# Weight tiles of 4352 bytes in place of 4224: where matmul operands begin in SBUF

## The chip, the cores and the metric

The kernel runs on one core of a Trainium2 chip. The metric is the time of one execution on the device in microseconds (us), where lower is better. The engines are named as the profile names them: PE is TensorE (matmuls), PEld its loading of weights, DVE is VectorE, ACT is ScalarE, POOL is GpSimd, SP is SyncE, which here only issues DMA transfers. SBUF is the on-chip memory of 128 partitions. An address below is a byte offset within a partition, and "remainder" is such an address modulo 256.

## The reference

The reference is one layer of an encoder block over 256 tokens of 2048 channels, in float32. Cut to its matrix products:

```python
hn = rmsnorm(h, mix_norm_pre)
proj = hn @ w_in                         # 2048 -> z 1024, xbc 1536, dt 32, u 1024
y_ssd = ssd_mixer(z, xbc, dt_raw, ...)   # bidirectional Mamba-2 scan, two chunks of 128 tokens
y_pool = pool_mixer(u, pool_w, pool_scale)
h = h + rmsnorm(concat(y_ssd, y_pool) @ w_out, mix_norm_post)
up = rmsnorm(h, ffn_norm_pre) @ w_ffn_up             # 2048 -> 2 x 5632
ff = (gelu(conv3(gate)) * val) @ w_ffn_down          # 5632 -> 2048
h = h + rmsnorm(ff, ffn_norm_post)
gate = sigmoid(rmsnorm(h, ple_norm_pre) @ w_ple_gate)    # 2048 -> 2048
h = h + rmsnorm(gate * (p @ w_ple), ple_norm_post)
```

## The kernel before

**Products in three parts.** TensorE multiplies operands of the type `float32r`, to which a float32 value is rounded. To keep the accuracy of float32, every weight matrix and every activation is split into a high part (the value rounded to `float32r`) and a low part (what is left), and a product is the sum of high x high, high x low and low x high. `split` (line 140) does it for weights: a raw weight tile arrives by DMA, ACT writes the high part with a copy (line 149), and DVE writes the low part with a subtraction (line 150).

**Where the parts lie.** `split` takes one tile for each part, from two groups of five buffers each in the pool `weights`: tag `whi` for high parts and `wlo` for low ones, 1056 float32 values (4224 bytes) a tile. 4224 is 16 x 256 + 128, so neighbouring buffers begin at remainders 128 apart. The built program before has them here:

| buffers | address of the first | remainders of the five |
|---|---|---|
| `raw` (3 of 8192 bytes) | 30560 | 96, 96, 96 |
| `whi` (5 of 4224 bytes) | 55136 | 96, 224, 96, 224, 96 |
| `wlo` (5 of 4224 bytes) | 76256 | 224, 96, 224, 96, 224 |
| pages (13 of 8192 bytes), `mid` (3 of 4096), `hs` (2 of 4096) | 97376 and up | 96 |
| `pth`, `ptl`, the gain tile | 18240 and up | 64 |
| `ident` | 16544 | 160 |

The two groups turn together, so the high and the low part of one weight tile always lie at opposite remainders: of 410 tiles that are split into these buffers, 246 have the high part at 96 and the low part at 224, and 164 the other way round. All other matmul operands that are split (the activation panels, the spare tiles below, `hs`) lie in pages or in `hs`, at remainder 96. Slices of operands begin at multiples of 512 bytes, with one exception: in the first projection (`dtu`) a tile's three slices begin 1408 bytes apart.

**Stages in order.** Two forms of product carry nearly all the time.

- Token-major (`token_major`, line 242): the activations are stationary (128 x 128), the weights are the moving operand, 512 columns at a time. It serves z, the output projection (`wo`, accumulators `woa`), the down-projection (`dn`, accumulators `dna`), ple and the gate (`gt`). A weight block is 256 rows by 1024 columns. Its products stand by tile, by half of the tokens `t`, by part `q`, and then by the two column halves, so that two products in a row use the same stationary operand. In the last block (and for the gate's second half in the last four) the order is by accumulator instead, and the stationary operand changes at every product. The down-projection does 13 of its 44 blocks with seven products in place of eight (`seven_products`, line 203; accumulators `dns` too): 21 matmuls instead of 24.
- Feature-major: the weights are stationary, the activations move. `feature_major` (line 270) does the `xbc` projection with 256 columns. `feature_pairs` (line 287) does the up-projection of the feed-forward (accumulators `ga` for the gate half, `va` for the value half; weight tiles named `ug` and `uv`): the panel `wox` holds the high and low parts of a slice side by side, so a high part of the weights is multiplied with 512 columns (high and low) and the low part with 256. A weight tile gives eight such pairs.

```python
mm(acc[f], wh[:, s], get.both(k), k == 0, False)
mm(acc[f][:, L:], wl[:, s], get(k)[0], False, k == NK - 1)
```

**Spare tiles.** In the second half of the gate, four weight tiles (two blocks) take their high and low parts from pages that are free by then (line 887): in the profile `gth` and `gtl`. They and the ordinary tiles of that stage (`gt_0h`, `gt_0l`, `gt_1h`, `gt_1l`) are multiplied with the same panel `dnx` in one unbroken series at the end.

**Order of the work.** The program is traced once, and a scheduler fixes each engine's order from dependences and buffers. Weights come by DMA from SP's queue into `raw`, three transfers ahead. Two more names in the change are `half_up`, a column of 0.5 that POOL uses at the very end (line 864), and `dynamic_dma_scratch_size`, the bytes at the start of SBUF that are set aside for descriptors of DMAs written by software (16384 when nothing is said).

Of the kernel before, what the change touches and what calls it, by code (L numbers as in the profile page):

```python
# [11 lines left out]
F32 = mybir.dt.float32  # L12
F32R = mybir.dt.float32r
# [3 lines left out]
P = 128  # L17
# [34 lines left out]
def build(nc, a, out):  # L52
# [5 lines left out]
    with tile.TileContext(nc) as tc, \  # L58
# [8 lines left out]
        def ins(r):  # L67
            return getattr(r, "ins", r)

        def page(name, dtype=F32):  # L70
            return gp.tile([P, 2048], dtype, tag="pg", bufs=13, name=name)
# [43 lines left out]
        def load(dst, src, ahead=False):  # L115

            with tc.issue_after(last["dma"]) if last and not ahead else nullcontext():
                return ins(nc.sync.dma_start(dst, src))
# [21 lines left out]
        def split(name, src, nel, cuts=()):  # L140

            if name in spare:
                hi, lo = spare.pop(name)
            else:
                hi = wp.tile([P, 1056], F32R, tag="whi", bufs=5, name=f"{name}h")
                lo = wp.tile([P, 1056], F32R, tag="wlo", bufs=5, name=f"{name}l")
            for c0, c1 in zip((0, *cuts), (*cuts, nel)):
                s = slice(c0, c1)
                last["act"] = ins(nc.scalar.copy(hi[:, s], src[:, s]))
                last["dve"] = ins(nc.vector.tensor_sub(lo[:, s], src[:, s], hi[:, s].bitcast(F32)))  # L150
            return hi, lo
# [51 lines left out]
        def seven_products(name, r, a_, acc, alt, start, stop):  # L203

            v = r.rearrange("p (b c) -> p b c", b=4)
            b11 = split(f"{name}a", r[:, :512], 512)
            b2 = split(f"{name}b", r[:, 1024:], 1024)

            nc.vector.tensor_sub(v[:, 0:2], v[:, 1::2], v[:, 0:2])
            nc.vector.tensor_sub(v[:, 3], v[:, 3], v[:, 0])
            nc.vector.tensor_sub(v[:, 2], v[:, 2], v[:, 3])
            t13 = split(f"{name}c", r[:, :1024], 1024)
            t42 = split(f"{name}d", r[:, 1024:], 1024)
            for x, (wh, wl), c, o, own in (
                    ("a11", b11, 0, alt[0], True), ("a12", b2, 0, acc[0][0], False), ("s4", b2, 512, acc[0][1], False),
                    ("s1", t13, 0, alt[1], True), ("s3", t13, 512, alt[2], True), ("a22", t42, 0, acc[1][0], False),
                    ("s2", t42, 512, alt[3], True)):
                xh, xl = a_[x]  # L220
                for q, (xx, ww) in enumerate(((xh, wh), (xh, wl), (xl, wh))):
                    mm(o, xx, ww[:, c:c + 512], own and start and q == 0, own and stop and q == 2)
# [111 lines left out]
        def row_rstd(name, src):  # L334

            r = []
            for t in range(2):
                q = tiny(f"{name}q{t}", 1)
                junk = page(f"{name}j{t}")
                nc.scalar.activation(junk, src[t], AF.Square, accum_out=q)  # L340
                r.append(rms(f"{name}{t}", [q], 1.0 / D))
            return r
# [86 lines left out]
        with tc.issue_after(half[0]), tc.issue_after(half[1]):  # L429
            xs_ = [page(f"x{t}") for t in range(2)]  # L430
            for t in range(2):
                load(xs_[t], x[t * P:(t + 1) * P, :])
            rx = row_rstd("rx", xs_)
            seg_w = page("seg_w", F32R)[:64, :].rearrange("p (a q s) -> p a q s", a=4, q=4)
            seg_x = page("seg_x", F32R)[:64, :].rearrange("p (a i l) -> p a i l", a=4, i=4)
            for a_ in range(4):
                nc.scalar.activation(seg_w[:32, a_], four[:32].unsqueeze(2).to_broadcast([32, 4, P]), AF.Copy,
                                     scale=-1.0)
                nc.scalar.copy(seg_x[32:, a_], among[32:].unsqueeze(2).to_broadcast([32, 4, P]))
            aneg = ep.tile([P, 32], F32, name="aneg")  # L440
            nc.scalar.activation(aneg, alog, AF.Exp)
            nc.gpsimd.tensor_scalar(aneg, aneg, -1.0, None, op0=ALU.mult)


            pt = page("pt")[:, :512].rearrange("p (k t) -> p k t", k=2)
            load(pt, a["p_t"])
            pth = cp.tile([P, 2, L], F32R, name="pth")
            ptl = cp.tile([P, 2, L], F32R, name="ptl")
            nc.scalar.copy(pth, pt)
            nc.vector.tensor_sub(ptl, pt, pth.bitcast(F32))  # L450
# [308 lines left out]
        h = [page(f"h{t}") for t in range(2)]  # L759
# [91 lines left out]
        vg = [page(f"vg{t}") for t in range(2)]  # L851
        sq = [[], []]

        half_up = cp.tile([P, 1], F32, name="half_up")
        nc.gpsimd.memset(half_up, 0.5)

        def rest_of(o):

# [88 lines left out]


# [14 lines left out]
```

## Time and profile before

| what | value |
|---|---|
| median of 3 runs | 1144.94 us (1144.43 to 1145.71) |
| profiled execution, first to last instruction (span) | 1144.3 us |
| mean granted clock of TensorE | 0.994 |
| busy PE / DVE / ACT / POOL | 1127.1 / 818.4 / 614.2 / 79.3 us |
| matmuls | 6049 records |
| up-projection of the feed-forward | 320 to 798 us of the span |
| down-projection | 798 to 1029 us |

The profile page and the views of the trace come from one execution, whose own time is its span; the page gives no other. In a row of the view in order of time stand the start (us from the span's start), the duration (us), the engine, the line, the operation, output <- inputs (buffer numbers left out), the shape and a count. Durations of matmuls overlap, so the distance from one start to the next says how fast PE goes on. Line 86 is the helper `mm`, through which all matmuls go; the tiles tell them apart.

### The profile page before, as it was taken

What the parts mean: (1) busy time and instruction counts of PE and PEld (TensorE: products, weight loads), DVE (VectorE), ACT (ScalarE), POOL (GpSimd) and SP (SyncE); (2) the same over time, 40 slices, a digit from 0 to 9 for tenths busy, and PEclk for the clock granted to TensorE, in tenths of its full rate; (3) what the DMA queues carried; (4) which work ended last, traced back from release to release, by engine and by line L of the source; (5) the groups of instructions that cost most, each with busy time, mean ns of one, the idle gap of its engine ahead of it and who ended that gap; (6) DMA issues with size and microseconds to landing.
All of it is one profiled execution on the core that took longest, in us unless ns stands there. A gap on an engine that the chain in (4) does not pass through costs nothing.

```text
span 1144.3 us, 15384 instructions
## 1 busy us (share of the span) xinstructions
PE 1127.1 (98%) x6049; PEld 970.4 (85%) x6049; DVE 818.4 (72%) x1067; ACT 614.2 (54%) x837; POOL 79.3 (7%) x91
## 2 busy tenths in 40 slices
PE   9999999999999999999999999999999999999996
PEld 9998888888888888888888888888888888887885
DVE  6659985754876666665766756668888888898573
ACT  6746543553674554554544545545655655667462
POOL 0201105200110000000000000000000000002001
PEclk9999999999999999999999999999999999999998
DMA  9942366556456555555555555556556746654752
GB/s 357 374 149 74 100 245 221 171 170 198 148 185 214 190 185 184 184 187 194 193 190 193 184 184 184 184 195 220 170 188 220 221 147 221 209 195 147 226 179 74
DMA packets 129592, 219.04 MB, mean 191 GB/s; under 512 B 3696, under 2 KB 96752, under 8 KB 128624
## 3 DMA queue, kind: packets, MB, share of 16 engines
q1 hardware_dynamic: 129232, 217.70, 57.2%
q8 instruction: 47, 0.77, 0.3%
q10 hardware_dynamic: 288, 0.36, 0.1%
q14 instruction: 25, 0.20, 0.0%
HBM read 215.95 MB, written 2.10 MB: 191 GB/s over the span
## 4 chain that ended last, share of the span: by engine, by line
PE 95%; DVE 2%; ACT 1%; POOL 1%; issue 1%; DMA 0%; POOLq 0%; DVEq 0%; ACTq 0%
PE va L86 21%; PE ga L86 21%; PE dna L86 17%; PE woa L86 8%; PE gt L86 7%; PE xbc L86 5%; PE dtu L86 4%; PE z L86 4%; PE dns L86 3%; PE pw L86 1%; PE ple L86 1%; PE yd L86 0%; DVE h L740 0%; PE seg L86 0%; DMA dtur<-w_in 0%
## 5 line engine op out<-in xcount | busy, mean ns | idle before, releaser
L86 PE MATMUL ga<-wox,ug_0h 128*128 128x512 f32 x352 | 125.5, 395 | 0.0
L86 PE MATMUL ga<-wox,ug_1h 128*128 128x512 f32 x352 | 125.1, 394 | 0.0
L86 PE MATMUL va<-wox,uv_0h 128*128 128x512 f32 x352 | 124.8, 393 | 0.0
L86 PE MATMUL va<-wox,uv_1h 128*128 128x512 f32 x352 | 124.8, 393 | 0.0
L86 PE MATMUL ga<-wox,ug_0l 128*128 128x256 f32 x352 | 99.1, 282 | 0.0
L86 PE MATMUL ga<-wox,ug_1l 128*128 128x256 f32 x352 | 99.1, 282 | 0.0
L86 PE MATMUL va<-wox,uv_0l 128*128 128x256 f32 x352 | 99.1, 281 | 0.0
L86 PE MATMUL va<-wox,uv_1l 128*128 128x256 f32 x352 | 99.1, 281 | 0.0
L86 PEld LDWEIGHTS va<-wox,uv_0h 128*128 128x128 f32 x352 | 66.1, 188 | 15.0
L86 PEld LDWEIGHTS va<-wox,uv_1h 128*128 128x128 f32 x352 | 66.1, 188 | 15.0
L86 PEld LDWEIGHTS ga<-wox,ug_1h 128*128 128x128 f32 x352 | 66.1, 188 | 14.9
L86 PEld LDWEIGHTS ga<-wox,ug_0h 128*128 128x128 f32 x352 | 66.1, 188 | 14.8
L86 PE MATMUL dna<-dn_0h,hs 128*128 128x512 f32 x248 | 75.8, 393 | 0.0
L86 PE MATMUL dna<-dn_1h,hs 128*128 128x512 f32 x248 | 75.6, 393 | 0.0
L86 PEld LDWEIGHTS ga<-wox,ug_0l 128*128 128x128 f32 x352 | 66.2, 188 | 0.1
L86 PEld LDWEIGHTS ga<-wox,ug_1l 128*128 128x128 f32 x352 | 66.2, 188 | 0.0
L86 PEld LDWEIGHTS va<-wox,uv_0l 128*128 128x128 f32 x352 | 66.2, 188 | 0.0
L86 PEld LDWEIGHTS va<-wox,uv_1l 128*128 128x128 f32 x352 | 66.2, 188 | 0.0
L781 POOL TENSOR_TENSOR fc<-fc,rfb 128x1024 f32<-128x1024 f32 x11 | 26.5, 2408 | 440.1 <-ACT fc L780 440.1
L86 PEld LDWEIGHTS dna<-dn_1h,hs 128*128 128x128 f32 x248 | 46.5, 188 | 10.8
L86 PEld LDWEIGHTS dna<-dn_0h,hs 128*128 128x128 f32 x248 | 46.5, 188 | 10.7
L86 PE MATMUL dna<-dn_0l,hs 128*128 128x512 f32 x124 | 40.2, 393 | 0.0
(1078 smaller groups left out, 2824.0 us busy)
## 6 DMA issues: line engine op xcount, KB each, us to landing
dn0r<-w_ffn_down SPq DMA_DIRECT2D x22, 1024.0 KB, 5.5
dn1r<-w_ffn_down SPq DMA_DIRECT2D x22, 1024.0 KB, 5.5
zr<-w_in SPq DMA_DIRECT2D x8, 1024.0 KB, 5.1
wo0r<-w_out SPq DMA_DIRECT2D x8, 1024.0 KB, 5.4
wo1r<-w_out SPq DMA_DIRECT2D x8, 1024.0 KB, 5.4
gt0r<-w_ple_gate SPq DMA_DIRECT2D x8, 1024.0 KB, 5.6
gt1r<-w_ple_gate SPq DMA_DIRECT2D x8, 1024.0 KB, 5.5
dtur<-w_in SPq DMA_DIRECT2D x14, 528.0 KB, 8.9
```

The source lines that it names most:

```text
L86: nc.tensor.matmul(o, lhsT, rhs, start=start, stop=stop, skip_group_check=True)
L781: nc.gpsimd.tensor_tensor(cv.rearrange("p (f t) -> p f t", f=4), cv.rearrange("p (f t) -> p f t", f=4), rfb.unsqueeze(1).to_broadcast([P, ...
```

## The change

The tiles of `whi` and `wlo` get 1088 values in place of 1056. A tile then takes 4352 bytes, 17 x 256, and all ten buffers begin at the same remainder. What is written to a tile and read from it stays: at most 1056 values. The ten tiles take 1280 bytes more; to make room, the software descriptors' area is halved to 8192 bytes, which moves every tile down. `half_up` (32 bytes with its padding) is taken from the pool of constants before `pth`, `ptl` and the gain tile and not after them, which leaves the remainder of everything behind the constants as it was and moves these three.

```diff
-                hi = wp.tile([P, 1056], F32R, tag="whi", bufs=5, name=f"{name}h")
-                lo = wp.tile([P, 1056], F32R, tag="wlo", bufs=5, name=f"{name}l")
+                hi = wp.tile([P, 1088], F32R, tag="whi", bufs=5, name=f"{name}h")
+                lo = wp.tile([P, 1088], F32R, tag="wlo", bufs=5, name=f"{name}l")
...
             load(pt, a["p_t"])
+            half_up = cp.tile([P, 1], F32, name="half_up")
+            nc.gpsimd.memset(half_up, 0.5)
             pth = cp.tile([P, 2, L], F32R, name="pth")
...
-        half_up = cp.tile([P, 1], F32, name="half_up")
-        nc.gpsimd.memset(half_up, 0.5)
...
-    nc = bacc.Bacc("TRN2", target_bir_lowering=False, num_devices=1)
+    nc = bacc.Bacc("TRN2", target_bir_lowering=False, num_devices=1, dynamic_dma_scratch_size=8192)
```

The addresses in the built program after:

| buffers | address of the first | remainders |
|---|---|---|
| `raw` | 22368 | 96 |
| `whi` | 46944 | 96, 96, 96, 96, 96 |
| `wlo` | 68704 | 96, 96, 96, 96, 96 |
| pages, `mid`, `hs` | 90464 and up | 96 |
| `pth`, `ptl`, the gain tile | 10080 and up | 96 |
| `ident` | 8352 | 160 |

No instruction changes its place on any engine, and none changes what it waits for. The one that the diff seems to move is the memset of `half_up`; on POOL it stood among the first instructions already. Before:

```order
L91 MEMSET mhalf 128x4
masks.py:197 MEMSET ident 128x128
L855 MEMSET half_up 128x1
masks.py:199 ISA
masks.py:199 AFFINE_SELECT ident<-ident 128x128
```

And after:

```order
L91 MEMSET mhalf 128x4
masks.py:197 MEMSET ident 128x128
L448 MEMSET half_up 128x1
masks.py:199 ISA
masks.py:199 AFFINE_SELECT ident<-ident 128x128
```

Only the line number differs.

## The prediction

> **What bounds the kernel.** I read the page first (busy shares, granted clock, chain), then PE's waits, then PE's rows in order of time, because a PE that is always busy can only become faster by shorter instructions.
>
> ```profile
> span 1144.3 us, 15384 instructions
> PE 1127.1 (98%) x6049; PEld 970.4 (85%) x6049; DVE 818.4 (72%) x1067; ACT 614.2 (54%) x837; POOL 79.3 (7%) x91
> PEclk9999999999999999999999999999999999999998
> q1 hardware_dynamic: 129232, 217.70, 57.2%
> q10 hardware_dynamic: 288, 0.36, 0.1%
> PE 95%; DVE 2%; ACT 1%; POOL 1%; issue 1%; DMA 0%; POOLq 0%; DVEq 0%; ACTq 0%
> ...
> L86 PE MATMUL ga<-wox,ug_0h 128*128 128x512 f32 x352 | 125.5, 395 | 0.0
> ...
> L86 PE MATMUL ga<-wox,ug_0l 128*128 128x256 f32 x352 | 99.1, 282 | 0.0
> ```
>
> PE is busy for 98% of the span at nearly full granted clock, and 95% of the chain is PE. Its longest waits are small and stand at changes of stage:
>
> ```profile
> PE gt L86 <- DVE gt_1l L150: 2.3, 1, 2.3
> PE xbc L86 <- DVE xb_0l L150: 2.0, 1, 2.0
> ```
>
> So the time is the number of matmuls times the distance between their starts, which I call the pitch. The duration in the page (395 ns) is no pitch, since matmuls overlap. The pitch has to be read from start times, over many instructions, since a row gives 0.01 us.
>
> The change touches only where operands begin. "Remainder" below is the byte address modulo 256. Before, the ten weight buffers begin at 96 and 224 in turn, and a tile's high and low parts always lie at opposite ones. Pages, panels and `hs` all begin at 96. If the remainder matters, the trace of before must show it already. It does, in two places.
>
> First, the up-projection (lines 770 to 789). Each weight tile feeds eight pairs of a 512-column product with its high part and a 256-column product with its low part, weights stationary. The rows are the first product of consecutive tiles; the built program has their high parts at 96, 224, 96, 224, 96:
>
> ```profile
> 561.09 0.39 PE L86 MATMUL va<-wox,uv_1h 128*128 128x512 f32 x1
> 563.87 0.39 PE L86 MATMUL va<-wox,uv_0h 128*128 128x512 f32 x1
> 566.68 0.39 PE L86 MATMUL va<-wox,uv_1h 128*128 128x512 f32 x1
> 569.46 0.39 PE L86 MATMUL va<-wox,uv_0h 128*128 128x512 f32 x1
> 572.28 0.39 PE L86 MATMUL va<-wox,uv_1h 128*128 128x512 f32 x1
> ```
>
> The tiles take 2.78, 2.81, 2.78 and 2.82 us: 347 ns a pair with the high part at 96, 352 with it at 224. Averaged over all whole tiles the same reading gives 347.0 (102 tiles) and 352.0 (68). Address alone makes 5 ns.
>
> Second, the last stage holds the only weights that lie at 96 in both parts: the spare tiles `gth` and `gtl`, which are pages. Their products alternate with those of ordinary tiles, on the same panel. First comes a run of 12 from spare tiles, then 12 from ordinary ones (the last row starts the next run):
>
> ```profile
> 1118.72 0.39 PE L86 MATMUL gt<-gth,dnxh 128*128 128x512 f32 x1
> ...
> 1121.44 0.39 PE L86 MATMUL gt<-gt_0h,dnxh 128*128 128x512 f32 x1
> ...
> 1124.20 0.39 PE L86 MATMUL gt<-gth,dnxh 128*128 128x512 f32 x1
> ...
> 1129.79 0.28 PE L86 MATMUL gt<-gtl,dnxh 128*128 128x256 f32 x1
> ...
> 1131.11 0.28 PE L86 MATMUL gt<-gt_0h,dnxh 128*128 128x256 f32 x1
> ```
>
> All operands alike: 2.72 us over 12, 226.7 ns each. Mixed: 2.76 over 12, 230.0 each. The 256-column products of the spare tiles, all alike, take 1.32 us over 11, 120.0 each. These are my prices of "after".
>
> **The change part by part.** *Token-major stages, 512 columns.* The weights are the moving operand here. The mean pitch before comes from the first and last row of an unbroken stretch:
>
> ```profile
> 149.76 0.63 PE L86 MATMUL z<-z_0h,hnh 128*128 128x512 f32 x2
> 171.48 0.63 PE L86 MATMUL z<-z_1h,hnl 128*128 128x512 f32 x2
> ...
> 229.94 0.48 PE L86 MATMUL woa<-wo_0h,cath 128*128 128x512 f32 x1
> 296.35 0.40 PE L86 MATMUL woa<-wo_1h,catl 128*128 128x512 f32 x1
> ...
> 798.41 0.63 PE L86 MATMUL dna<-dn_0h,hs 128*128 128x512 f32 x2
> 1028.90 0.40 PE L86 MATMUL dna<-dn_0l,hs 128*128 128x512 f32 x1
> ```
>
> z: 94 pitches in 21.72 us (the second row merges two products and begins with the first), 231.1. wo: 287 in 66.41, 231.4. dn: 998 in 230.49, 231.0 (what lies between two rows is counted in the order of the program). The code issues 192, 384 and 1017 of them, and the gate stage 300 beside the spare ones; gate is priced as z.
>
> - dn: 1017 x (231.0 - 226.7) = 4.4 us.
> - wo: 384 x 4.7 = 1.8 us.
> - z and gate: 492 x 4.4 = 2.2 us.
>
> *Up-projection.* It issues 1408 pairs (four groups of 352 as quoted). By the built program 848 have the high part at 96 and 560 at 224, so the mean is (848 x 347.0 + 560 x 352.0) / 1408 = 349.0. No row shows a pair with all three operands alike. I bound it by the nearest rows, within one tile at 224 (starts of its first three 512-column products, and the next tile's):
>
> ```profile
> 563.87 0.39 PE L86 MATMUL va<-wox,uv_0h 128*128 128x512 f32 x1
> 564.21 0.40 PE L86 MATMUL va<-wox,uv_0h 128*128 128x512 f32 x1
> 564.57 0.40 PE L86 MATMUL va<-wox,uv_0h 128*128 128x512 f32 x1
> ```
>
> Its first pair takes about 0.34 us and its second about 0.36; the recorded starts in nanoseconds have 346 and 358, and later ones 352, 347, 351, 353, 358, 352. So the pitch there wanders, while a tile at 96 holds 346 to 348 throughout. Ends: 345 (lowest seen) and 358 (highest). I take 226.7 + 120.0 = 346.7, the sum of the two alike runs, because both of those hold one steady value, and so does the 347.0 tile; the wandering appears only where the high part is off. Gain: 1408 x (349.0 - 346.7) = 3.2 us, with ends of +5.6 and -12.7.
>
> *256-column products with alike operands.* Here the price goes up:
>
> ```profile
> 52.78 0.36 PE L86 MATMUL xbc<-hnh,xb_0h 128*128 128x256 f32 x1
> 64.15 0.28 PE L86 MATMUL xbc<-hnh,xb_1l 128*128 128x256 f32 x1
> 0.00:52.00 52.00, 49.87 (x302) 49.25 (x303) 31.54 (x42) 38.91 (x56) 7.01 (x16) 1.00 0.98 364
> ```
>
> 95 pitches in 11.37 us, 119.7 against 120.0: 576 x 0.3 is 0.2 us lost, and about 0.1 more for the gate stage's shorter products.
>
> *First projection (`dtu`).* Its slices begin 1408 bytes apart, which is 5 x 256 + 128, so the middle one stays off the others. The last row above, a stretch with its DMA share (0.98) and GB/s at the end, says that the DMA engines set this stage. Nothing taken.
>
> *Scratch, `half_up`, tile sizes.* The two DMA kinds quoted above that move data are hardware ones; nothing is issued that the halved scratch serves, so it costs 0. The memset keeps its place on POOL, and its new address moves `pth`, `ptl` and the gain tile from remainder 64 to 96; the 48 products of ple are too few to price. Tiles are larger by unused bytes: no instruction reads more. No instruction and no wait moves.
>
> *Cover.* A faster PE needs weights sooner. The tightest place in dn is this one:
>
> ```profile
> 891.68 1.22 DVE L150 TENSOR_TENSOR dn_1l<-dn0r,dn_1h 128x1024 fp32r<-128x1024 f32 x1
> 894.97 0.39 PE L86 MATMUL dna<-dn_1l,hs 128*128 128x512 f32 x1
> 798.00:1029.00 231.00, 231.00 (x1003) 187.76 (x1002) 200.86 (x240) 137.39 (x172) 0.91 (x2) 1.00 0.60 196
> ```
>
> The low part is ready at 892.90 and used at 894.97, 2.07 us later. VectorE is busy 200.9 of 231 us in dn, and would be so for 200.9 of 226.6. By the same two kinds of rows its lead swings between 2.1 and 8.4 us with a period of three weight blocks (24 + 24 + 21 products), over which PE gains 69 x 4.3 = 0.3 us. So the cover holds; if it did not, VectorE would be late next.
>
> **Sum.** 4.4 + 1.8 + 2.2 + 3.2 - 0.3 = 11.3 us off the span of 1144.3. The median of the runs, 1144.94, lies 0.6 above that span; I take the same off it: 1133.6.
>
> A rule speaks against all this. The Trainium skill, "SBUF — State Buffer", section "Who interferes with whom", gives TensorE two independent read ports, one for the moving operand and one for the weight load, and says that PE never waits on anyone; its section "Operand start alignment" calls the element-size rule one of legality and says that its runs timed nothing. By that rule the time would stay at 1144.9. The trace disagrees: 347 against 352 ns for the same products.
>
> **The rivals.**
> - *Up-projection gains nothing.* The alike pair settles near today's mean of 349.0. For: its 512- and 256-column products alternate, as in no alike run. Time 1144.9 - 8.1 = 1136.8.
> - *Up-projection takes the wandering pitch.* In the tiles at 224 the low part lies at 96, as it will in all tiles, and its load runs beside the 512-column stream at 96. All pairs at 352.0: 1408 x 3.0 = 4.2 lost, 1141.0. Against: the high part's load then also lies at 96, as in the steady tiles.
> - *Slower: the up-projection locks onto the bad phase.* Each pair takes 358, the worst of the wandering ones: 1408 x 9.0 = 12.7 lost against 8.1 gained, 1149.5. The whole change loses from a pair of 349.0 + 8.1 / 1.408 = 354.8 on, and by over 0.2% from 356.4.
> - *The two-column order does not hold 226.7.* The spare run changes its stationary operand at every product; most of dn, wo, z and gate uses one for two columns. Only the up-projection gains: 1142.
> - *The remainder does nothing* and the 5 ns come from which buffer it is: 1144.9. Against: three different buffers at 96 read the same 347.
>
> **How the numbers follow.** The forecast gets 0.55: of the four regular patterns read above that change weights at every product or pair, three hold a steady pitch (512 alike, 256 alike, high part at 96) and one wanders. No gain in the up-projection gets 0.15, the wandering pitch 0.13, no hold in two-column order 0.05, no effect 0.07, slower 0.05. A difference of 0.2% (2.3 us) is about what runs of this kernel tell from none (they lie within 1.3 us). Faster by more: 0.55 + 0.15 + 0.13 + 0.05 = 0.88; same 0.07; slower 0.05. The first three cases hold 0.83, so the range runs from the 345 end of the up-projection (2.4 us below the forecast, rounded in to 1131.5) to 1141.5.
>
> **What would show it.** In the profile of after: dn from its first to its last product some 4.4 us shorter, at 226.7 a product; the stretch of wo likewise; tiles of the up-projection all equal, near 2.77 us (2.82 means the wandering pitch, 2.86 the bad phase); xbc at 120; PE's waits unchanged. I am wrong if the ordinary tiles of the gate stage still differ from the spare ones, or if a wait of PE for VectorE appears in dn.

## The result: 1142.4 us, and two groups of times

The changed kernel has a median of 1142.39 us over 18 executions (1133.63 to 1144.54); the kernel before, run beside it, has 1144.88 us (1144.26 to 1147.81). The ratio of the two sets is 0.9967 with an interval of 0.9953 to 0.9981 (the medians alone give 0.9978): faster by 0.2 to 0.3%, and not by the 1% that was forecast. The forecast of 1133.6 and its upper end of 1141.5 both lie below the median.

The 18 times do not spread evenly. Three are 1133.63, 1134.11 and 1135.15; the other fifteen lie from 1141.54 to 1144.54; nothing lies between. The forecast is the time of the smaller group. The profiled execution belongs to it: its time is 1133.63 us at a span of 1131.8. First its page: spans, busy shares, granted clock by slice, and the chain.

```profile
span 1131.8 us, 15384 instructions
PE 1115.5 (99%) x6049; PEld 964.9 (85%) x6049; DVE 817.4 (72%) x1067; ACT 613.8 (54%) x837; POOL 79.6 (7%) x91
PEclk9999999999999999999999999999999999999998
PE 95%; DVE 2%; ACT 1%; POOL 1%; issue 1%; POOLq 0%; DVEq 0%; ACTq 0%
```

As many instructions as before, as much work on DVE, ACT and POOL, and 11.6 us less on PE. PE's rows in order of time show the ends of the three stretches read in the prediction (z, wo, dn), of xbc, and of two runs of 12 at the end of the gate stage:

```profile
52.13 0.36 PE L86 MATMUL xbc<-hnh,xb_0h 128*128 128x256 f32 x1
63.61 0.28 PE L86 MATMUL xbc<-hnh,xb_1l 128*128 128x256 f32 x1
...
147.87 0.40 PE L86 MATMUL z<-z_0h,hnh 128*128 128x512 f32 x1
169.21 0.62 PE L86 MATMUL z<-z_1h,hnl 128*128 128x512 f32 x2
...
227.00 0.47 PE L86 MATMUL woa<-wo_0h,cath 128*128 128x512 f32 x1
292.18 0.39 PE L86 MATMUL woa<-wo_1h,catl 128*128 128x512 f32 x1
...
791.05 0.63 PE L86 MATMUL dna<-dn_0h,hs 128*128 128x512 f32 x2
1017.31 0.39 PE L86 MATMUL dna<-dn_0l,hs 128*128 128x512 f32 x1
...
1106.27 0.39 PE L86 MATMUL gt<-gth,dnxh 128*128 128x512 f32 x1
...
1108.99 0.39 PE L86 MATMUL gt<-gt_0h,dnxh 128*128 128x512 f32 x1
...
1111.71 0.39 PE L86 MATMUL gt<-gth,dnxh 128*128 128x512 f32 x1
```

With the same counts of pitches as before: z 21.34 us / 94 = 227.0 ns (before 231.1), wo 65.18 / 287 = 227.1 (231.4), dn 226.26 / 998 = 226.7 (231.0), and xbc 11.48 / 95 = 120.8 (119.7). At the end of the gate stage 12 products of spare tiles and 12 of ordinary tiles now take 2.72 us alike, 226.7 ns each; the ordinary ones took 230.0 before.

The up-projection is best read from the chain, which puts 128 products of `ga` or of `va` (64 pairs) into a row. Of the kernel before and then of the changed one, start, length and what:

```profile
351.86 22.33 PE ga L86 x128
```

```profile
325.29 22.19 PE va L86 x128
347.48 22.19 PE ga L86 x128
```

22.33 us over 64 pairs are 348.9 ns; 22.19 are 346.7. So in this execution the two large terms of the forecast are there. What the forecast misses is in the executions that the profile doesn't show.

### The profile page after: what moved, and what is told of

Read it like the earlier page. It is cut to its first block, busy times and chain, and to the rows that moved or that the text cites. A ratio compares the mean times of both kernels' runs of the same rounds, so it can differ in the third digit from the quotient of the medians.

```text
span 1131.8 us, 15384 instructions
## 1 busy us (share of the span) xinstructions
PE 1115.5 (99%) x6049; PEld 964.9 (85%) x6049; DVE 817.4 (72%) x1067; ACT 613.8 (54%) x837; POOL 79.6 (7%) x91
## 4 chain that ended last, share of the span: by engine, by line
PE 95%; DVE 2%; ACT 1%; POOL 1%; issue 1%; POOLq 0%; DVEq 0%; ACTq 0%
PE va L86 22%; PE ga L86 21%; PE dna L86 17%; PE woa L86 8%; PE gt L86 7%; PE xbc L86 5%; PE dtu L86 4%; PE z L86 4%; PE dns L86 3%; PE pw L86 1%; PE ple L86 1%; PE yd L86 0%; DVE h L742 0%; PE seg L86 0%; PE mx L86 0%
```

## The experiments

All experiments start from the changed kernel, and are compared with runs of the kernel before on the same chip (medians of 1144.49 to 1144.55; 1143.4 in one execution beside the two kernels that were run once each). A time is 1.8 us longer than the span of the same execution, within 0.1 us in every run here.

**The changed kernel once more, for a profile of the larger group.** No edit.

> The changed kernel, unchanged. Its 18 timed executions fell in two groups, 3 at 1133.6 to 1135.2 and 15 at 1141.5 to 1144.5 us, and the profiled one (span 1131.8) belongs to the first. Theory A (the alike layout has two steady patterns of matmul pitch, and something at the start of an execution decides which): the times fall in the same two groups again; an execution of the upper group has no new waits of PE, but a longer pitch in a whole stage (either dn, wo, z and gate at about 231 in place of 226.7 ns, or the up-projection's pair at about 352 in place of 346.7; each would make about 8 us). Theory B (waits): the pitches are those of the first profile in both groups, and PE waits some 8 us more in the upper one. Theory C (the granted clock): the upper group shows a lower granted clock by 0.7%.

Twelve executions: 1131.97, 1132.15, 1132.24, 1132.27, 1135.09, 1135.93, and then 1141.54, 1141.57, 1141.63, 1141.78, 1142.83, 1144.98. The median is 1138.73, the ratio 0.9937 (0.9913 to 0.9961). Over both sets 9 of 30 executions fall in the lower group by their times. This time the profiled one is of the upper group (1142.83 us). Its waits of PE, and the chain in its up-projection:

```profile
PE gt L86 <- DVE gt_1l L150: 2.3, 1, 2.3
PE xbc L86 <- DVE xb_0l L150: 2.0, 1, 2.0
...
PE rfbp L86 <- DVE rfbw L350: 0.5, 1, 0.5
```

```profile
span 1141.0 us, 15384 instructions
...
326.87 22.62 PE va L86 x128
349.49 22.61 PE ga L86 x128
```

The waits are those of the other trace, but for 0.3 us at `dtu`. Both profiled executions have a mean granted clock of 0.996. But a pair of the up-projection now takes 22.61 / 64 = 353.3 ns, in every row, where the other execution of the same program takes 346.7. The token-major stretches are the same in both:

```profile
801.59 0.64 PE L86 MATMUL dna<-dn_0h,hs 128*128 128x512 f32 x2
...
1027.90 0.39 PE L86 MATMUL dna<-dn_0l,hs 128*128 128x512 f32 x1
```

226.31 us over 998 pitches, 226.8 ns. So the distance between the groups lies in one place, the up-projection. The two traces differ in two more places, which nearly cancel. In the one of the upper group the granted clock drops for a few microseconds in the stage of xbc; below is this stretch of it, then the same stretch of the other trace. The number in brackets behind the first busy time counts PE's products, and the third number from the end is the granted clock:

```profile
137.00:142.00 5.00, 5.00 (x31) 5.00 (x31) 5.00 (x11) 1.08 (x2) 0.00 (x0) 0.66 0.34 93
```

```profile
137.00:142.00 5.00, 5.00 (x43) 5.00 (x43) 5.00 (x11) 1.05 (x1) 0.00 (x0) 1.00 0.35 95
```

Twelve products fewer, and the time from the first product of xbc to the first of z is 97.2 us in place of 95.7. The trace of the lower group has such a drop in the gate stage instead (0.72 from 1032 to 1038 us), and its gate products take 91.8 us in place of 90.4. Over the 30 executions the mean granted clock orders the times within each group: 1132.0 to 1132.3 at 0.998, 1133.6 to 1134.1 at 0.996 and 1135.1 to 1135.9 at 0.994 in the lower one; 1141.5 to 1142.0 at 0.997, 1142.8 to 1143.5 at 0.996 and 1144.4 to 1145.0 at 0.995 in the upper one. It doesn't tell the groups apart: at 0.996 there are times of 1134 and of 1143.

The sums of the two groups, by the rows of the prediction: 1144.9 - 8.1 + 1408 x (353.3 - 349.0) = 1142.9 for the upper one, 1144.9 - 8.1 - 1408 x (349.0 - 346.7) = 1133.6 for the lower; measured 1141.5 to 1145.0 and 1132.0 to 1135.9.

The two traces also show where the up-projection parts. The up-projection's products run without a gap once the scale of the block's norm (`rfb`) is known; just ahead of that, PE waits for `rfbw`, and then puts two rows of transpositions `rfbp` among the products. In the execution of the lower group:

```profile
313.97 0.46 PE L86 MATMUL rfbp<-ident,rfbw 128*128 128x128 f32 x2 [0.52 <-DVE rfbw L350]
...
316.14 0.49 PE L86 MATMUL rfbp<-ident,rfbw 128*128 128x128 f32 x2
316.38 0.47 PE L86 MATMUL ga<-wox,ug_0h 128*128 128x512 f32 x1
...
316.81 0.40 PE L86 MATMUL ga<-wox,ug_1h 128*128 128x512 f32 x1
...
317.16 0.39 PE L86 MATMUL ga<-wox,ug_1h 128*128 128x512 f32 x1
...
317.50 0.40 PE L86 MATMUL ga<-wox,ug_1h 128*128 128x512 f32 x1
```

And in that of the upper group:

```profile
315.38 0.46 PE L86 MATMUL rfbp<-ident,rfbw 128*128 128x128 f32 x2 [0.52 <-DVE rfbw L350]
...
317.55 0.49 PE L86 MATMUL rfbp<-ident,rfbw 128*128 128x128 f32 x2
317.79 0.48 PE L86 MATMUL ga<-wox,ug_0h 128*128 128x512 f32 x1
...
318.23 0.40 PE L86 MATMUL ga<-wox,ug_1h 128*128 128x512 f32 x1
...
318.59 0.40 PE L86 MATMUL ga<-wox,ug_1h 128*128 128x512 f32 x1
...
318.94 0.40 PE L86 MATMUL ga<-wox,ug_1h 128*128 128x512 f32 x1
```

The second row of `rfbp` begins 2.17 us after the first in both. From then on the starts of the 512-column products (the 256-column ones between them are left out above) are 0.43, 0.35 and 0.34 us apart in the one and 0.44, 0.36 and 0.35 in the other, and so they stay for some 1370 pairs: the first product of dn is 474.7 us behind the 316.38 in the one and 483.8 behind the 317.79 in the other, 9.1 us or 6.7 ns a pair. In the recorded starts in nanoseconds the lower group repeats every two pairs (233 + 117 + 231 + 113, within 1 ns), the upper every three (241 + 120 + 235 + 114 + 232 + 118). These are two patterns of one and the same stream, each steady once it is there.

**Is it the entry that decides? A nudge ahead of each block.** If so, a product put between two blocks of the up-projection should make the choice anew. The edit adds one transposition that nobody reads ahead of blocks 1 to 10:

```diff
         for s in range(DFF // 512):
+            if s:
+                nc.tensor.transpose(misc(f"again{s}")[:, :P], ident, ident)
```

> The changed kernel with one more product, a 128 x 128 transposition that nobody reads, ahead of each of the blocks 1 to 10 of the up-projection (44 products more in PE's rows at most, some 0.1 to 0.3 us each, 1 to 3 us in all). Theory A': each nudge shifts the phase, so the blocks of one execution need no longer share one pattern: a trace shows blocks near 346.7 and blocks near 353.3 ns a pair, and the times lie between the two groups. Rival (a state that holds for a whole execution): all blocks of a trace show one pitch, and the times form the same two groups.

Median 1138.94 us (1137.52 to 1139.85), ratio 0.9945 (0.9932 to 0.9959). The four times lie together, between the groups. The chain of one execution:

```profile
325.59 22.61 PE va L86 x128
348.20 0.11 PE again L774
348.31 22.19 PE ga L86 x128
370.50 22.19 PE va L86 x128
392.69 0.11 PE again L774
392.80 22.61 PE ga L86 x128
415.41 22.62 PE va L86 x128
```

Here 22.61 and 22.19 stand side by side in one execution, and the length changes only at a nudge. Of the eleven blocks five (1, 4, 6, 8, 10) take 346.7 a pair and six take 353.3. So the pattern is no state of the chip or of a whole execution: in this trace it is chosen where the stream is broken, and holds until the next break. What makes the choice at a break stays open. By sum: 1136.8 + 1408 x (350.3 - 349.0) + 10 x 0.11 = 1139.7 for this execution; its time was 1139.85.

**Without the alternation: the eight high products of a tile, then the eight low ones.**

```diff
+                    for part in range(2):
                         for kk in range(4):
...
+                                if part == 0:
+                                    mm(acc[f], wh[:, s], get.both(k), k == 0, False)
+                                else:
+                                    mm(acc[f][:, L:], wl[:, s], get(k)[0], False, k == NK - 1)
```

> The changed kernel with another order in the up-projection alone: of each weight tile first all eight 512-column products with the high part, then all eight 256-column ones with the low part. Theory A', from the two traces of the changed kernel: all its other stages hold one pitch in both, and only the alternation of 512 and 256 columns has two steady patterns (one of two pairs at 347.0, one of three pairs at 353.3 ns a pair, 9 us in all), chosen by the phase in which the stage is entered after the wait for the tokens' factors at some 320 us. Without the alternation the streams are uniform: eight products at 226.7 and eight at 120, 2.77 us a tile but for the turns, one group of times at 1132 to 1136. Rival (a state of the chip, not of the order): two groups about 9 us apart as before.

One group: 1136.11, 1136.29, 1137.68, 1137.94, 1138.07; ratio 0.9934 (0.992 to 0.9947). That part came as expected. The time is higher than the lower group's, because a pair costs more than the sum of the two alike runs:

```profile
325.95 22.35 PE va L86 x128
```

349.2 ns a pair: the 512-column products take 230 on average, the 256-column ones 119. In the recorded starts the eight high products of a tile take 233, 236, 228, 233, 231, 227, 226 and 227 ns: the 226.7 of the token-major stages comes only with the sixth. The five times lie within 2 us of each other, but just above the lower group of the changed kernel. **The order high, high, low, low** (the same loop over `part`, inside the one over `kk`) lies between:

> As the order high-then-low, but in small: two 512-column products, then the two 256-column ones on the same rows of the activation. Theory A': another alternation, so another set of steady patterns; between 346.7 and 353 ns a pair, and one or more groups of times between 1132 and 1143. It shows whether the uniform streams of eight are needed.

1134.66, 1134.80, 1138.37, 1139.16 (median 1136.58, ratio 0.9927, 0.991 to 0.9945). The profiled execution, that of 1139.16, has this chain:

```profile
328.60 22.29 PE va L86 x128
```

348.3 a pair. In it the second row of `rfbp` begins at 319.61, 3.5 us later than in the lower group's trace: the first product of xbc begins 1.9 us later (0.7 of it a wait at `dtu`), and xbc takes the 1.5 us more that go with the drop of the granted clock. 1133.6 + 3.5 + 1370 x 1.6 ns = 1139.3 accounts for its time of 1139.16. What sets the two of 1134.7 apart stays open.

**What the change did of itself: the small tiles, with all else moved.** Tiles of 1056 values again, with the smaller scratch area and `half_up` ahead, as in the change.

```diff
-                hi = wp.tile([P, 1088], F32R, tag="whi", bufs=5, name=f"{name}h")
-                lo = wp.tile([P, 1088], F32R, tag="wlo", bufs=5, name=f"{name}l")
+                hi = wp.tile([P, 1056], F32R, tag="whi", bufs=5, name=f"{name}h")
+                lo = wp.tile([P, 1056], F32R, tag="wlo", bufs=5, name=f"{name}l")
```

> The changed kernel with tiles of 4224 bytes again: only the moved start of SBUF, half_up and the remainder of pth, ptl and the gain tile are left of the change. Both theories: 1144.9 within 1 us, with up-projection tiles of 347 and 352 ns a pair in turn; if it is faster by more, the moves and not the tile size made it.

1144.77 us (1144.58 to 1146.06), ratio 1.0001 (0.9992 to 1.001), and the tiles of the up-projection read 347.0 and 352.0 ns a pair in turn, as before. The moves and the scratch area are worth nothing; the remainder makes the whole change.

**Must all be alike, and alike to what?** Three kernels shift the buffers as a whole. The first puts 128 bytes between the groups, so that all high parts lie at 96 and all low parts at 224; the second puts the 128 bytes ahead of both, so that all weights lie at 224 and the panels stay at 96; the third shifts everything by 160 bytes, so that all operands are alike at 0. A part of the first one's edit (the tile `pad1` stands between the two groups, and a second such tile behind them leaves the pages at 96):

```diff
-        spare = {}
+        spare, pads = {}, {}
...
+                if "pad1" not in pads:
+                    pads["pad1"] = wp.tile([P, 32], F32, name="pad1")
+                    nc.gpsimd.memset(pads["pad1"], 0.0)
```

> All high parts at remainder 96 and all low parts at 224 (tiles of 4352 bytes, 128 bytes of padding ahead of the low ones), all else as after. It differs from after in the low parts alone. If the pitch follows the remainders as the profile of before showed, every pair of the up-projection takes 347 ns (the tile at 96 of before) and the token-major stages alternate 226 and 234 or worse, about 230 to 231: 1408 x 2.0 = 2.8 us less than before, about 1142. Theory A: this mixed layout has one group of times only, as before has. Theory B: two groups here too.

> All ten weight buffers at remainder 224, pages and panels at 96: weights alike among themselves, but opposite to the other operand. If it is the likeness of the two operands of one product and of the weight load beside it that counts, the token-major stages do not hold 226.7 and the time is not below 1141. If only likeness from one product to the next counts (no change of remainder along a stream), dn, wo, z and gate run at 226.7 and the time is about 1134 to 1137.

> The changed kernel moved by 160 bytes as a whole: weights, pages, panels and hs at remainder 0 in place of 96. If likeness is what counts and not the value, all is as in the changed kernel: dn, wo, z at 226.7, two groups of times at 1132 to 1136 and 1141.5 to 1145. If the place within 256 bytes counts, the uniform pitch changes.

High at 96 and low at 224: 1141.97 us (1141.21 to 1145.69), ratio 0.9978 (0.9968 to 0.9988). Its profiled execution, which is the slowest of its ten, has the first row below; the second is of the kernel with all weights at 224, at 1150.66 us (1149.14 to 1151.1), ratio 1.0045 (1.0031 to 1.0059); the third of the one with all at 0, whose four times are 1134.18, 1134.23, 1135.11 and 1142.91 (ratio 0.9926, 0.9897 to 0.9955):

```profile
328.65 22.40 PE va L86 x128
```

```profile
331.04 22.47 PE va L86 x128
```

```profile
325.54 22.61 PE va L86 x128
```

All at 0 behaves as all at 96: the same two groups, 353.3 a pair in the profiled execution, that of 1142.91, and 226.7 in dn. So these two values of the remainder are worth the same. In the token-major stages it is the likeness of the operands that meet in a product that counts, and not that of one weight to the next: with all weights alike at 224, and the activations at 96, the products take 232.4 (z, dn) to 233.6 (wo), more than the mixed 231.0 of before, and a pair of the up-projection 351.1. Distances other than 128 bytes were not tried in these stages. High at 96, low at 224 reads 231.6 in dn, and 350.0 a pair in the profiled execution, which was expected at 347. Eight of its ten times lie lower, at 1141.2 to 1142.7; at the same granted clock of 0.997 the distance is 4.3 us (1145.69 against 1141.30 and 1141.36), which is what 347 would give (1408 x 3.0 = 4.2). No trace of such an execution was kept, so that two patterns explain it too is argued, not shown; the table below has both 346.7 and 350.0 for this layout.

**The price of each offset.** Two more kernels, run once each, let each half-block of the up-projection (22 of them, 64 pairs each) place its high and low parts at other offsets in their buffers, in order in the one and shuffled in the other. The rest of the kernel is unchanged.

```diff
-        def split(name, src, nel, cuts=()):
+        def split(name, src, nel, cuts=(), at=(0, 0)):
...
+                hi, lo = hi[:, at[0]:at[0] + nel], lo[:, at[1]:at[1] + nel]
...
-                feature_pairs(f"ug{s}{i}", w_up, s * 512 + i * 256, hf, ga)
+                feature_pairs(f"ug{s}{i}", w_up, s * 512 + i * 256, hf, ga, AT[2 * s])
```

> The changed kernel, but each of the 22 halves of the up-projection's blocks (64 pairs each) puts its high and low parts at another place within 256 bytes of their buffers: high part at +0 and low part at +0, 16, 32 ... 240 bytes in turn, then six other combinations. One trace reads a pitch for each combination. Theory A' (the pattern follows from where the three operands lie and from the phase): each half shows one steady pattern of its own; +0/+0 shows 346.7 or 353.3, +0/+128 some 347 to 350 as in the layout of before and in high-at-96-low-at-224. A combination that holds 346.7 or less whatever stood before it is what a faster kernel needs. Rival (only likeness modulo 256 matters, all unlike ones are alike): all combinations but +0/+0 and the two with equal places show the same pitch.

> The same combinations in another order of the halves. Where a combination reads the same in both, its pattern does not hang on what stood before; where it reads two values, it does. I expect +0/+0 and at least some others to differ between the two, by up to 7 ns a pair, and +0/+128 to read 347 to 350 in both.

They took 1136.79 and 1136.34 us. The ns per pair, by the offset of the high and the low part in bytes (0 is the remainder 96 of the panel), read from the recorded starts over the last 56 of the 64 pairs. The first half-block of each kernel holds the breaks at `rfbp`; its values, marked with a star, are of the 20 to 24 pairs behind them:

| high, low | in order | shuffled |
|---|---|---|
| 0, 0 | 353.3* | 346.7 |
| 0, 16 to 80 (five steps of 16) | 346.7 | 346.7 |
| 0, 96 | 351.7 | 346.7 |
| 0, 112 | 346.7 | 346.7 |
| 0, 128 | 346.7 | 350.0* |
| 0, 144 | 351.1 | 346.7 |
| 0, 160; 0, 176; 0, 192 | 351.1; 350.0; 351.1 | 351.1; 350.0; 351.0 |
| 0, 208; 0, 224; 0, 240 | 348.9; 353.3; 346.7 | 348.9; 353.3; 346.7 |
| 64, 0 | 350.0 | 340.1 |
| 64, 64 | 353.3 | 353.3 |
| 128, 0; 128, 64; 128, 128 | 351.9; 346.6; 351.2 | 352.0; 346.7; 351.0 |
| 192, 0 | 340.0 | 340.0 |

Seventeen of the 22 read the same in both orders, within 0.2 ns. Five (0, 0; 0, 96; 0, 128; 0, 144; 64, 0) read two values: these have two patterns, and the offset alone doesn't set which one holds. Two equal readings don't show that an offset has one pattern only. And all alike is not the best. With the high part 192 bytes on, a pair takes 340.0 (227 + 113).

**That offset for the whole up-projection.** The high parts begin 192 bytes on, at remainder 32; the low parts and the panel stay at 96.

```diff
-        def feature_pairs(name, w, c0, get, acc):
+        def feature_pairs(name, w, c0, get, acc, at=(48, 0)):
```

> The changed kernel with the high parts of the up-projection's weight tiles 192 bytes further on in their buffers (remainder 32; low parts and panel at 96). In both runs with mixed places this combination read 227 + 113 = 340.0 ns a pair, whatever stood before it. If that holds for a whole stage: 1408 x 6.7 = 9.4 us below the lower group of the changed kernel and 18.7 below the upper one, so 1122 to 1126, in one group of times. If it was an accident of two entries (the mirror combination, +64 and +0, read 340.0 in one run and 350.0 in the other), the times fall in two groups again, some 14 us apart.

1123.14, 1123.19, 1124.90, 1125.28, 1126.54 and 1138.43; the median is 1125.09 us, the ratio 0.9842 (0.9803 to 0.9881). The chain of one execution:

```profile
326.92 21.76 PE va L86 x128
348.68 21.76 PE ga L86 x128
```

340.0 a pair. The sum 1136.8 - 1408 x (349.0 - 340.0) = 1124.1 is met. The one execution at 1138.43 is 13.2 to 13.5 us longer than the two others at its granted clock of 0.996; 1408 x 10 ns = 14.1 us, as between the two values of (64, 0), would about account for it, but no trace shows it. So the one group of times that was expected did not quite come. **The same offset for xbc too:**

> As e11, with the high parts of the xbc projection's weights 192 bytes further on as well (576 products of 256 columns, 120 ns each when alike). If 113 ns is to be had there too, up to 576 x 7 = 4.0 us less than e11, less what the stage's waits take back; if 113 needs the alternation with 512 columns, the same as e11 within 1 us.

1123.09, 1124.66, 1125.59, 1125.90 (median 1125.13, ratio 0.982, 0.9804 to 0.9836). In the trace:

```profile
52.37 0.36 PE L86 MATMUL xbc<-hnh,xb_0h 128*128 128x256 f32 x1
63.65 0.28 PE L86 MATMUL xbc<-hnh,xb_1l 128*128 128x256 f32 x1
```

11.28 us over 95 pitches, 118.7 where the change has 120.8. Over 576 products that is 1.2 us at most, and the times don't tell it from the kernel without it: the 113 does not come here without the alternation with 512 columns. These two kernels are the fastest of this study, 1.6 to 1.8% ahead of the kernel before.

## Why the prediction was wrong, point by point

- **Token-major stages** (8.1 us): right. 231 became 226.7 to 227.1 in z, wo and dn, in executions of both groups, and the ordinary tiles of the gate stage no longer differ from the spare ones. The rival that the two-column order would not hold this fell.
- **Moves, scratch area, `half_up`:** right at nothing; the kernel with these alone reads 1.0001.
- **256-column products:** right in sign, small in size: 1.1 ns lost on xbc where 0.3 were taken, 0.6 us in all. The 120.0 was right: past the first 24 products the changed kernel holds it. The 119.7 of before is a mean with the start of the stage in it, and 120.0 was a price without one.
- **Cover in dn:** right. No wait of PE for VectorE appears in dn: the waits of PE name no tile of it, before or after, and DVE's work in the stage stays at 201 us:

```profile
790.00:1018.00 228.00, 228.00 (x1010) 188.75 (x1009) 201.04 (x242) 137.80 (x173) 0.91 (x2) 1.00 0.61 198
```

- **Up-projection** (3.2 us): this step failed. I took "226.7 + 120.0 = 346.7, the sum of the two alike runs, because both of those hold one steady value". 346.7 exists, in 9 of 30 executions by their times. In 21 of 30 the pair takes 353.3, steadily as well, and 1408 x 4.3 = 6.1 us are lost in place of 3.2 gained (one execution of each kind has a trace). The reason failed at "one": that each of two products holds one pitch on its own doesn't give their alternation one pitch. The kernel without the alternation has one group in its five executions; with it there are two. It also failed at "sum", and that the lower group reads 346.7 to the tenth is luck: its products take 231.7 and 115.0 ns on average, those of the upper group 236.4 and 117.0, and neither has 226.7 and 120.0. The sign of this was in the quoted rows: tiles at 224 wandered between 346 and 358 within a tile. I read that as the mark of unlike operands and gave "the wandering pitch" 352.0 and 1141.0 us. Of the cases that change the up-projection's price it was the nearest, right in kind (the alternation is not the sum of the alike runs) and 1.4 us short of the median. The bad phase was nearer in mechanism, since the stream does lock onto one of several patterns, but at 353.3 and not at 358. The 1142 of the two-column rival is nearest in number, for a reason that the runs refute.
- **The range:** its upper end stood 0.9 us below the median, since I placed the third case at exactly 352.0, with no width of its own.
- **The time against the span:** I took them 0.6 us apart; every execution has 1.8. The profiled execution of before was thus a slightly slow one (about 1146.1 us, at a granted clock of 0.994). The forecast takes no harm from this, since its sum comes to the median of before less 11.3 us.
- **The rule weighed against the trace:** the Trainium skill, "SBUF — State Buffer", section "Who interferes with whom", says that PE never waits on anyone. The prediction read this as a rule by which no placement would matter. So read, the runs disagree: 226.7 against 232.4 ns in dn for the same products with weights at 96 and at 224, and 340.0 to 353.3 a pair by offset. Whether PE waits on anything in these cases no run shows.

## What to carry to other kernels

Where PE is busy all the time, read the pitch from start times, and sort it by where the operands begin: a few nanoseconds on thousands of products are the whole difference between kernels. Prices of two uniform runs don't add up to the price of their alternation; and one profiled execution can show one of several steady patterns, so look at the list of all times for groups before a term is read from a trace. Alike addresses are a guess, not a rule: a table of offsets, a half-block each within one kernel, took two executions and found what neither version had.

## What the runs showed of the hardware that I had not expected

- One program, the same waits within 0.3 us and the same mean granted clock, yet a stretch of 475 or 484 us: a stream of alternating 512- and 256-column products settles after a break into one of two repeating patterns and keeps it until the next break (22.19 and 22.61 us for 64 pairs, changing only at a nudge).
- With offsets between the operands a pair takes 340.0 to 353.3 ns, in steps that don't grow with the distance.
- Weights that are alike among themselves and 128 bytes off the activations (modulo 256) are worse than mixed ones: 232.4 against 231.0 ns in dn, 1150.7 us against 1144.9.
- What in the chip makes the patterns isn't settled by these runs, and neither is what decides which one an entry takes.
